# The first mixture's rows that go by DRAM: plain gathers into ring places and adds on VectorE in place of adding gathers

## The chip, the cores and the metric

The kernel runs on one core of a Trainium2 chip. The time is device microseconds of one execution. A core has TensorE (matrix products into PSUM), VectorE, ScalarE and GpSimd (called PE, DVE, ACT and POOL in the profile), SyncE (SP), which here issues most transfers, and sixteen DMA engines that all queues share. Every engine and every queue works through its own instructions in order and waits on semaphores for the others.

## What is computed

Two transformer blocks follow one another on 512 rows of width 1024: in each a mixer, then a mixture of experts, then a norm. The change is in the mixture of the first block: every row picks one of 4 groups and in it 2 of 8 experts, so there are 32 experts of width 256.

```python
combine = jnp.sum(jax.nn.one_hot(global_idx, N_EXPERTS, dtype=jnp.float32) * weights[..., None], axis=1)
y = jnp.zeros_like(x2d)
for e in range(N_EXPERTS):
    h = jax.nn.silu(x2d @ w_gate[e]) * (x2d @ w_up[e])
    y = y + combine[:, e:e + 1] * (h @ w_down[e])
```

The block's output is its input plus y.

## The kernel before, in words

`moe1` computes this mixture. Experts go in pairs, 16 units of two; each expert has 64 slots for rows, so a unit fills 128 partitions. Unit u gathers its rows from DRAM (L1596), turns them by transposes (L1609), multiplies them by its gate and up matrices (L1711), takes silu on ScalarE (L1714) and the product on VectorE (L1715), transposes the result (L1765, copied at L1766) and, one unit later in the code, multiplies it by the down matrices (L1655). Two matrices of each kind, 1 MB each, are loaded per unit, 96 MB in all. The residual `h` lies in SBUF as four tiles of 128 rows.

A unit's result rows reach `h` in one of two ways:

- By TensorE: `down` splits the rows into a high part (ScalarE, L1785) and a low part (VectorE, L1786), and `scatter` multiplies a one-hot matrix (L1790) by them (L1806, L1807) and adds the outcome to `h` on VectorE (L1800), half a tile at a time, through two PSUM banks in turn.
- By DRAM: `by_dram` scales the rows on ScalarE (L1664), and an indirect DMA of GpSimd's queue writes them to their places in a DRAM buffer `yd` (L1665), which is zeroed early in the first mixer (L503). After the last such unit eight indirect DMAs (L1730, one for each of the two choices of each of the four tiles) read rows of `yd` and add them to `h` in flight. A row whose expert is not among these units has an index out of bounds, and nothing is moved for it.

`FROM` (the first expert by DRAM, 8) and `BYDRAM` (20 experts) make units 4 to 13 go by DRAM.

The matrices come through a ring of places of 1 MB. Its parts have 6, 6, 3 and 2 places; `mo.cycle` says which part each next load takes, 17 loads to a cycle, and `place` takes a place outside of the cycle. Within a part the places go round. A load is issued on SyncE's queue, and it waits there, with all that is queued behind it, until its place has been read for the last time. A planner orders the instructions of each engine by its own model of when things are ready, so the order on a queue can differ from the code.

After unit 15 comes a loop for extra rounds (L1589), for experts that got more rows than they have slots. It starts with a meeting of all engines and queues. The down product of unit 15 and the last scatters come behind it.

```python
for u in range(mo.U):
    ...
    if prev and prev[0] in far:
        by_dram(*prev)
```

Of the kernel before, what the change touches and what calls it, by code (L numbers as in the profile page):

```python
# [16 lines left out]
T = 512  # L17
# [9 lines left out]

FROM = {1: 8, 2: 0}
BYDRAM = {1: 20, 2: 14}
# [153 lines left out]
class Kern:  # L183
# [259 lines left out]
    def mixer1(self, after):  # L443
# [52 lines left out]
        for step in "R00 R01 P0 R10 R11 A0 P1 R20 R21 A1 P2 R30 R31 A2 P3 A3".split():  # L496
            kind, j = step[0], int(step[1])
            if kind == "P":
                qkv[j] = self.sb_proj(pp, sp, j, xh, xl)
                if j == 2:  # L500
                    self.yd = tc.dram_tile([ZROW[1], D], F32, name="yd1")
                    zeros = qkv[j][0][64:128, 0]
                    nc.sync.dma_start(self.yd.rearrange("(p a) (d c) -> p (a d) c", p=64, c=T),  # L503
                                      zeros[:, None, :].to_broadcast([64, ZROW[1] // 32, T]))
                if j == 3:
                    wo = shift_pools()
            elif kind == "A":
                self.sb_attn(sp, j, qkv.pop(j), o, ("sb",))
            else:
                g = int(step[2])  # L510
                unit = self.rw_unit(up, j, g, S[g], o, AR, bt, kt, vch, xg, g2, TTc, PC)
                next(unit)
                drain(before)
                next(unit)
                before = unit
                if (j, g) == (3, 1):
                    drain(unit)
                    cA.close()
# [909 lines left out]
    def places(self, rp, mo):  # L1428
# [10 lines left out]
        nc.vector.tensor_tensor(rw, rw, mo.pos, OP.add)  # L1439
        nc.vector.tensor_tensor(rw, rw, ov, OP.add)  # L1440
        if mo.which == 2:
            nc.vector.tensor_scalar(mo.row, rw, float(ZROW[2]), None, op0=OP.min)
            return
        nc.vector.tensor_copy(mo.row, rw)

# [197 lines left out]
    def moe1(self):  # L1643
# [34 lines left out]
        def body(num, wts, idx, first):  # L1678
# [14 lines left out]
            for u in range(mo.U):  # L1693
# [3 lines left out]
                last = u == mo.U - 1  # L1697
                if last and first:
                    SC = self.place(mo, 2, R32)
                    y14 = down(prev[1], [self.moe_next(mo) for _ in range(2)], wts[:, u - 1:u], onehot(u - 1, SC[:, 0:T]),  # L1700
# [26 lines left out]
                if far and u == far[-1] + 1:  # L1727
                    for c in range(2):
                        for n in range(NT):
                            nc.gpsimd.indirect_dma_start(  # L1730
                                out=self.h[:, n], out_offset=None, in_=self.yd,
                                in_offset=bass.IndirectOffsetOnAxis(ap=mo.row[:, n, c:c + 1], axis=0),
                                bounds_check=ZROW[1] - 1, oob_is_err=False, compute_op=OP.add)
                hT = gp.tile([128, 2, 128], F32, name="hT", bufs=1)
# [48 lines left out]
    def rows_hl(self, oh, ol, p, w):  # L1783

        self.last = self.nc.scalar.activation(oh, p, AF.Copy, scale=w)  # L1785
        self.lo = self.nc.vector.scalar_tensor_tensor(ol, p, w, oh, op0=OP.mult, op1=OP.subtract)  # L1786

    def onehot(self, SC, mo, num, u):
# [37 lines left out]
    def moe2(self, out):  # L1826
        nc, tc, mo = self.nc, self.tc, self.mo
        with mo.cx, mo.cr:
# [48 lines left out]
            def body(num, wts, idx, first):  # L1877
# [50 lines left out]
                if first:  # L1928
                    back = [self.moe_slot(mo) for _ in range(NT)]
                    for n in range(NT):  # L1930
                        for c in range(2):
                            nc.gpsimd.indirect_dma_start(
                                out=back[n][:, c * D:c * D + D], out_offset=None, in_=self.yd,
                                in_offset=bass.IndirectOffsetOnAxis(ap=mo.row[:, n, c:c + 1], axis=0),
                                bounds_check=ZROW[2], oob_is_err=False)
                g = self.moe_slot(mo)[:, 0:D]
# [103 lines left out]
```

## Time and profile before

| | us |
|---|---|
| median of 3 runs | 1421.97 (1419.99 to 1422.15) |
| the profiled execution, its own time | 1419.69 |
| its span | 1417.9 |
| TensorE busy | 1289.0 (91%) |
| VectorE busy | 841.6 (59%) |
| ScalarE busy | 701.6 (49%) |
| GpSimd busy | 410.2 (29%) |

The durations below come from the one profiled execution; its time stands 2.28 us under the median. Times on its axis count from the start of the span. The mixture of the first block lies between about 460 and 722 us. "busy" counts instructions only: the landing of a DMA is told apart, and a row in brackets says how long the engine was idle before and what ended it. DMA share is the mean busy share of the sixteen DMA engines. PEclk is the granted clock of TensorE as a share of 2.4 GHz.

### The profile page before, as it was taken

How to read it: one execution, taken by the hardware profiler on the slowest of the kernel's cores; microseconds unless marked ns; L12 is line 12 of the kernel's file. 1: busy time of each engine (PE TensorE's matmuls, PEld its weight loads, DVE VectorE, ACT ScalarE, POOL GpSimd, SP SyncE). 2: the span in 40 equal slices, each digit the busy share in tenths (PEclk: the TensorE clock that was granted, in tenths of full speed). 3: DMA queues.
4: the chain of work that ended last, by engine and by line, in shares of the span. 5: the costliest groups of instructions: out<-in, count | busy, mean ns of one | idle time of the engine just before them, and what ended most of it. 6: DMA issues, size and time to landing. Idle time of an engine off the chain costs nothing.

```text
span 1417.9 us, 20482 instructions
## 1 busy us (share of the span) xinstructions
PE 1289.0 (91%) x7792; PEld 927.7 (65%) x7792; DVE 841.6 (59%) x1432; ACT 701.6 (49%) x1217; POOL 410.2 (29%) x329
## 2 busy tenths in 40 slices
PE   7999999999897999999379999999996999999993
PEld 5777766767696555554156776777894666666662
DVE  4679866566656131000075656657637799998895
ACT  6433433334634221211064555555545788888883
POOL 1000224241104101110366102011124555555445
PEclk9999999999998899999789999999997999999996
DMA  5232440000484999999832121202386999889943
GB/s 189 75 89 75 107 109 2 1 1 2 188 330 170 386 419 419 418 418 422 223 101 75 30 76 45 86 24 100 105 334 209 321 360 382 320 332 391 385 166 125
DMA packets 54452, 283.93 MB, mean 200 GB/s; under 512 B 8849, under 2 KB 9745, under 8 KB 28738
## 3 DMA queue, kind: packets, MB, share of 16 engines
q1 hardware_dynamic: 43634, 254.75, 47.9%
q0 software_dynamic: 9840, 26.39, 5.8%
q8 instruction: 66, 1.08, 0.3%
q10 hardware_dynamic: 864, 1.31, 0.3%
q14 instruction: 48, 0.39, 0.1%
HBM read 270.70 MB, written 22.29 MB: 207 GB/s over the span
## 4 chain that ended last, share of the span: by engine, by line
PE 68%; DVE 13%; DMA 11%; ACT 3%; issue 2%; POOL 1%; SPq 0%; DVEq 0%; POOLq 0%; ACTq 0%
PE mm L322 12%; PE ua L1903 4%; PE ua L1901 4%; PE ua L1902 4%; PE mm L1711 4%; DMA ew<-in_e1down_dram 3%; DMA ew<-in_e1up_dram 3%; PE ua L1655 2%; PE sb L322 2%; PE sb L1844 2%; PE sb L1843 2%; PE sb L1845 2%; PE sb L715 2%; DMA ew<-in_e1gate_dram 2%; DVE elo L1625 2%
## 5 line engine op out<-in xcount | busy, mean ns | idle before, releaser
L1625 DVE TENSOR_TENSOR elo<-ew,ehi 128x1024 fp32r<-128x1024 f32 x147 | 231.1, 1614 | 32.9 <-ACT ehi L1624 22.6
L1624 ACT ACTIVATE ehi<-ew 128x1024 fp32r<-128x1024 f32 x192 | 203.0, 1061 | 62.7 <-PE ua L1902 37.2
L322 PE MATMUL mm<-xh,whi 128*128 128x512 f32 (+1 forms) x384 | 155.9, 406 | 4.0 <-DVE hq L1143 3.7
L322 PE MATMUL mm<-xl,whi 128*128 128x512 f32 (+1 forms) x384 | 154.0, 401 | 0.5 <-DVE xl L354 0.3
L322 PE MATMUL mm<-xh,wlo 128*128 128x512 f32 (+1 forms) x384 | 152.8, 398 | 0.0
L1625 POOL TENSOR_TENSOR elo<-ew,ehi 128x1024 fp32r<-128x1024 f32 x45 | 125.9, 2799 | 64.8 <-ACT ehi L1624 63.0
L1711 PE MATMUL mm<-ew,xTh 128*64 128x256 f32 x1024 | 119.2, 386 | 6.4 <-DMA ew<-in_e1up_dram 4.7
L1903 PE MATMUL ua<-elo,xTh 128*96 128x512 f32 x256 | 102.9, 402 | 8.5 <-DVE elo L1625 8.4
L1711 PEld LDWEIGHTS mm<-ew,xTh 128*64 128x64 f32 x1024 | 73.5, 139 | 47.5 <-DMA ew<-in_e1up_dram 6.4
L1715 DVE TENSOR_TENSOR hh<-hh,mm 128x256 f32<-128x256 f32 x16 | 6.7, 421 | 163.5 <-ACT hh L1714 163.5
L1901 PE MATMUL ua<-ehi,xTh 128*96 128x512 f32 x256 | 102.3, 399 | 0.7 <-ACT xTh L1613 0.6
L1902 PE MATMUL ua<-ehi,xTl 128*96 128x512 f32 x256 | 101.8, 398 | 0.0
L296 ACT ACTIVATE whi<-w 128x1024 fp32r<-128x1024 f32 x53 | 55.9, 1057 | 91.1 <-PE mm L322 72.5
L297 DVE TENSOR_TENSOR wlo<-w,whi 128x1024 fp32r<-128x1024 f32 x52 | 63.7, 1227 | 51.7 <-ACT whi L296 51.5
L1596 POOL DMA_INDIRECT xg<-xd,idx x32 | 36.7, 1147 | 196.2 <-PE sb L1609 123.7
L322 PEld LDWEIGHTS mm<-xh,whi 128*128 128x128 f32 x384 | 73.4, 191 | 23.2 <-DVE hq L1143 5.4
L322 PEld LDWEIGHTS mm<-xl,whi 128*128 128x128 f32 x384 | 73.7, 192 | 16.7 <-issue 3.5
L322 PEld LDWEIGHTS mm<-xh,wlo 128*128 128x128 f32 x384 | 73.6, 192 | 16.0 <-issue 2.2
L1655 PE MATMUL ua<-ew,hT 128*64 128x512 f32 x240 | 66.4, 600 | 1.2 <-ACT hT L1766 1.1
L1714 ACT ACTIVATE hh<-mm 128x256 f32<-128x256 f32 x16 | 6.1, 383 | 112.8 <-PE mm L1711 112.8
L1903 PEld LDWEIGHTS ua<-elo,xTh 128*96 128x96 f32 x256 | 41.9, 164 | 30.6 <-DVE elo L1625 11.2
L1167 POOL TENSOR_TENSOR hAT<-hAT,hmt 128x512 f32<-128x512 f32 x16 | 22.1, 1381 | 118.9 <-DVE hmt L1166 118.3
(640 smaller groups left out, 3028.0 us busy)
## 6 DMA issues: line engine op xcount, KB each, us to landing
ew<-in_e1up_dram SPq DMA_DIRECT2D x32, 1024.0 KB, 17.8
ew<-in_e2up_dram SPq DMA_DIRECT2D x32, 1024.0 KB, 8.3
ew<-in_e2gate_dram SPq DMA_DIRECT2D x32, 1024.0 KB, 9.2
ew<-in_e2down_dram SPq DMA_DIRECT2D x32, 1024.0 KB, 12.5
ew<-in_e1gate_dram SPq DMA_DIRECT2D x31, 1024.0 KB, 19.5
ew<-in_e1down_dram SPq DMA_DIRECT2D x30, 1024.0 KB, 20.6
w<-in_win_dram SPq DMA_DIRECT2D x53, 512.0 KB, 3.6
ew<-in_wout_dram SPq DMA_DIRECT2D x8, 1024.0 KB, 6.9
```

The costliest lines, as they stand in the source:

```text
L296: nc.scalar.activation(hi, s, AF.Copy)
L297: (eng or nc.vector).tensor_tensor(lo, s, hi, OP.subtract)
L322: mm = lambda w, x, start=False, stop=False: nc.tensor.matmul(p[:, s], w[:, k], x[:, k, s], start=start, stop=stop, skip_group_check=parts ...
L715: nc.tensor.matmul(po[d, 0:128], v[:, kb, d], wT[hh][:, kb * 128:(kb + 1) * 128], start=kb == 0, stop=kb == b)
L1596: return self.nc.gpsimd.indirect_dma_start(out=xg, out_offset=None, in_=mo.xd, in_offset=bass.IndirectOffsetOnAxis(ap=idx[:, u:u + 1], axi ...
L1624: self.hi = nc.scalar.activation(hi, s, AF.Copy)
L1625: self.lo = (nc.gpsimd if pool else nc.vector).tensor_tensor(lo, s, hi, OP.subtract)
L1655: nc.tensor.matmul(p[hs(a)], hT[:, k, hs(a)], w[a][:, k * 1024 + d * 512:k * 1024 + d * 512 + 512], start=k == 0, stop=k == 1)
L1711: nc.tensor.matmul(d[hs(a)], xT[:, k, hs(a)], w[2 * m + a][:, k * 256:k * 256 + 256], start=k == 0, stop=k == KD - 1)
L1901: nc.tensor.matmul(p, xh[:, kk], hi[:, s], start=kk == 0, stop=False)
L1902: nc.tensor.matmul(p, xl[:, kk], hi[:, s], start=False, stop=False)
L1903: nc.tensor.matmul(p, xh[:, kk], lo[:, s], start=False, stop=kk == KD - 1)
```

## The change

`FROM` of the first mixture becomes 6, so units 3 to 12 go by DRAM and unit 13 goes by TensorE; the number of units on each way is as before. `yd` gets one row more, which two small DMAs set to zero, and an index out of bounds is clamped to that row (`places`), so all rows are moved. The return is taken over by `back`, which the second mixture now shares: plain gathers, each into half of a landing tile. In the first mixture the landing tiles are two places of ring part 2 and two of ring part 3, taken in unit 13. In unit 14 VectorE adds both halves of each tile to `h`. The scatter of unit 13 stands ahead of unit 14's down product.

```diff
-FROM = {1: 8, 2: 0}
+FROM = {1: 6, 2: 0}
...
-                    self.yd = tc.dram_tile([ZROW[1], D], F32, name="yd1")
+                    self.yd = tc.dram_tile([ZROW[1] + 1, D], F32, name="yd1")
                     zeros = qkv[j][0][64:128, 0]
-                    nc.sync.dma_start(self.yd.rearrange("(p a) (d c) -> p (a d) c", p=64, c=T),
+                    for d in range(2):
+                        nc.sync.dma_start(self.yd[ZROW[1]:ZROW[1] + 1, T * d:T * d + T], zeros[0:1])
+                    nc.sync.dma_start(self.yd[0:ZROW[1]].rearrange("(p a) (d c) -> p (a d) c", p=64, c=T),
                                       zeros[:, None, :].to_broadcast([64, ZROW[1] // 32, T]))
...
+        nc.vector.tensor_scalar(mo.row, rw, float(ZROW[mo.which]), None, op0=OP.min)
         if mo.which == 2:
-            nc.vector.tensor_scalar(mo.row, rw, float(ZROW[2]), None, op0=OP.min)
             return
-        nc.vector.tensor_copy(mo.row, rw)
...
                 if last and first:
+                    self.scatter(ys[-1:], 0)
+                    self.scatter(ys[-1:], 1)
...
                 if far and u == far[-1] + 1:
-                    for c in range(2):
-                        for n in range(NT):
-                            nc.gpsimd.indirect_dma_start(
-                                out=self.h[:, n], out_offset=None, in_=self.yd,
-                                in_offset=bass.IndirectOffsetOnAxis(ap=mo.row[:, n, c:c + 1], axis=0),
-                                bounds_check=ZROW[1] - 1, oob_is_err=False, compute_op=OP.add)
+                    back = self.back(mo, [self.place(mo, i) for i in (2, 2, 3, 3)])
+                if far and u == far[-1] + 2:
+                    for n in range(NT):
+                        for c in range(2):
+                            nc.vector.tensor_tensor(self.h[:, n], self.h[:, n], back[n][:, c * D:c * D + D], OP.add)
...
+    def back(self, mo, tiles):
+
+        for n, t in enumerate(tiles):
+            for c in range(2):
+                self.nc.gpsimd.indirect_dma_start(
+                    out=t[:, c * D:c * D + D], out_offset=None, in_=self.yd,
+                    in_offset=bass.IndirectOffsetOnAxis(ap=mo.row[:, n, c:c + 1], axis=0),
+                    bounds_check=ZROW[mo.which], oob_is_err=False)
+        return tiles
```

SyncE's queue, the loads of the last units before (the names are ring places of part 0 to 3 with a running number; DMAHW and DMASW are the semaphores of transfers issued by SyncE and by GpSimd): the down pair of unit 12, gate, up and down of the units 14 and 13, the down pair of unit 14, gate of unit 15.

```order
L1540 DMA ew2_5659<-in_e1down_dram 128x2048 [waits DMAHW2_49,PE_49]
L1540 DMA ew2_5661<-in_e1down_dram 128x2048 [waits DMAHW3_49,PE_49]
L1540 DMA ew2_5684<-in_e1gate_dram 128x2048 [waits DMAHW4_49,PE_49]
L1540 DMA ew3_5686<-in_e1gate_dram 128x2048 [waits DMAHW5_49,PE_49]
L1540 DMA ew0_5688<-in_e1up_dram 128x2048 [waits DMAHW6_49,PE_49]
L1540 DMA ew0_5690<-in_e1up_dram 128x2048 [waits DMAHW7_49,PE_49]
L1540 DMA ew0_5741<-in_e1down_dram 128x2048 [waits DMAHW0_49,PE_49]
L1540 DMA ew0_5743<-in_e1down_dram 128x2048 [waits DMAHW1_49,PE_49]
L1540 DMA ew1_5791<-in_e1down_dram 128x2048 [waits DMAHW2_49,PE_49]
L1540 DMA ew1_5793<-in_e1down_dram 128x2048 [waits DMAHW3_49,PE_49]
L1540 DMA ew1_5811<-in_e1gate_dram 128x2048 [waits DMAHW4_49,PE_49]
```

The same place on SyncE now, again from the down pair of unit 12 to the first gate matrix of unit 15.

```order
L1541 DMA ew2_5643<-in_e1down_dram 128x2048 [waits DMAHW4_49,PE_49]
L1541 DMA ew2_5645<-in_e1down_dram 128x2048 [waits DMAHW5_49,PE_49]
L1541 DMA ew0_5700<-in_e1up_dram 128x2048 [waits DMAHW6_49,PE_49]
L1541 DMA ew0_5702<-in_e1up_dram 128x2048 [waits DMAHW7_49,PE_49]
L1541 DMA ew0_5753<-in_e1down_dram 128x2048 [waits DMAHW0_49,PE_49]
L1541 DMA ew0_5755<-in_e1down_dram 128x2048 [waits DMAHW1_49,PE_49]
L1541 DMA ew2_5696<-in_e1gate_dram 128x2048 [waits DMAHW5_49,DMAHW2_49,PE_49]
L1541 DMA ew1_5821<-in_e1down_dram 128x2048 [waits DMAHW3_49]
L1541 DMA ew1_5823<-in_e1down_dram 128x2048 [waits DMAHW4_49]
L1541 DMA ew3_5698<-in_e1gate_dram 128x2048 [waits DMASW2_49,DMASW1_49,DVE_49]
L1541 DMA ew1_5841<-in_e1gate_dram 128x2048 [waits DMAHW6_49]
```

Unit 14's two gate matrices moved behind its up matrices and the down pair of unit 13; the first (part 2) waits for the load and the use of the second down matrix of unit 12, whose place it takes (5645), the second (part 3) for two gathers and VectorE, which are the writers and the reader of the third landing tile (5665).

VectorE before, from unit 13's product to unit 15's, with the one-hots, the low parts and a small copy between.

```order
L1715 TENSOR_TENSOR hh_5643<-hh_5643,mm_5610 128x256 [waits Activation_49]
L1790 TENSOR_SCALAR ew2_5790<-io512_4406,num_3848 128x512 [waits DMAHW2_49,DMAHW1_49,DMAHW7_49,DMAHW0_49,PE_49]
L1790 TENSOR_SCALAR ew2_5790<-io512_4406,num_3848 128x512
L1715 TENSOR_TENSOR hh_5725<-hh_5725,mm_5692 128x256 [waits Activation_49]
L1746 COPY ew2_5855<-wts_3849 128x1 [waits DMAHW4_49,DMAHW3_49,DMASW2_49]
L1786 SCALAR_TENSOR_TENSOR ew2_5796<-ua_5797,wts_3849,ew2_5796 128x512 [waits DMAHW3_49,Activation_49]
L1786 SCALAR_TENSOR_TENSOR ew2_5796<-ua_5804,wts_3849,ew2_5796 128x512 [waits Activation_49]
L1715 TENSOR_TENSOR hh_5852<-hh_5852,mm_5819 128x256 [waits Activation_49]
```

VectorE now, from the first add after unit 13's product (5663 to 5666 are the four landing tiles; 1802 is the one-hot, 1788 the low part, 1812 the eviction of a scatter).

```order
L1735 TENSOR_TENSOR h_3258<-h_3258,ew2_5663 128x1024 [waits DMASW5_49]
L1735 TENSOR_TENSOR h_3258<-h_3258,ew2_5663 128x1024 [waits DMASW6_49,DVE_49]
L1802 TENSOR_SCALAR ew2_5820<-io512_4408,num_3850 128x512 [waits DMAHW4_49,DMAHW3_49,DMAHW5_49,DMASW2_49,DVE_49]
L1735 TENSOR_TENSOR h_3258<-h_3258,ew2_5664 128x1024 [waits DMASW7_49]
L1802 TENSOR_SCALAR ew2_5820<-io512_4408,num_3850 128x512
L1735 TENSOR_TENSOR h_3258<-h_3258,ew2_5664 128x1024 [waits DMASW0_49,DVE_49]
L1788 SCALAR_TENSOR_TENSOR oh0_5759<-ua_5760,wts_3851,oh0_5759 128x512 [waits Activation_49]
L1735 TENSOR_TENSOR h_3258<-h_3258,ew3_5665 128x1024 [waits DMASW1_49]
L1788 SCALAR_TENSOR_TENSOR oh1_5767<-ua_5768,wts_3851,oh1_5767 128x512 [waits DMASW4_49,DMASW2_49,Activation_49]
L1735 TENSOR_TENSOR h_3258<-h_3258,ew3_5665 128x1024 [waits DMASW2_49,DVE_49]
L1735 TENSOR_TENSOR h_3258<-h_3258,ew3_5666 128x1024 [waits DMASW3_49]
L1812 TENSOR_TENSOR h_3258<-h_3258,ch_5788 128x512 [waits PE_49]
```

The eight adds stand ahead of unit 14's product, which comes after the evictions of unit 13's scatter; the last add follows this first eviction.

TensorE now, the scatter of unit 13 (the banks ch and pq) and the gate product of unit 14, whose second matrix is 5698.

```order
L1819 MATMUL ch_5788<-oh0_5759,SC_5757 128x512 [waits DVE_49]
L1819 MATMUL pq_5792<-oh0_5759,SC_5757 128x512
L1818 MATMUL ch_5796<-oh0_5759,SC_5757 128x512 [waits DVE_49]
L1819 MATMUL ch_5796<-oh0_5759,SC_5757 128x512
L1818 MATMUL pq_5800<-oh0_5759,SC_5757 128x512 [waits DVE_49]
L1819 MATMUL pq_5800<-oh0_5759,SC_5757 128x512
L1818 MATMUL ch_5804<-oh1_5767,SC_5757 128x512 [waits DVE_49,Activation_49]
L1819 MATMUL ch_5804<-oh1_5767,SC_5757 128x512
L1818 MATMUL pq_5808<-oh1_5767,SC_5757 128x512 [waits DVE_49]
L1819 MATMUL pq_5808<-oh1_5767,SC_5757 128x512
L1818 MATMUL ch_5812<-oh1_5767,SC_5757 128x512 [waits DVE_49]
L1714 MATMUL mm_5704<-ew3_5698,xTh_5630 64x256 [waits DMAHW5_49]
```

Before, unit 14's gate and up products stood ahead of unit 13's down product, and no scatter stood between; now they come behind it and behind six and a half of the eight scatters of unit 13.

## Rows read from the trace of the kernel before

**Rows 1.** Busy time by stretches: stretch, us, engines busy (instructions), granted clock, DMA share, GB/s.

```profile
660.00:680.00 20.00, 16.42 (x94) 7.82 (x90) 1.41 (x4) 3.40 (x6) 1.18 (x2) 1.00 1.00 418
680.00:700.00 20.00, 7.78 (x64) 4.60 (x64) 0.99 (x2) 0.77 (x2) 12.22 (x8) 0.84 0.93 227
```

**Rows 2.** The chain that ended last, 670 to 715 us: start, us, what.

```profile
675.07 7.85 DMA yd<-ot,out
...
687.53 19.46 DMA h<-yd,row
707.00 1.62 issue
708.62 6.25 PE ua L1655 x16
```

**Rows 3.** Timeline of TensorE and ScalarE: start, us, engine, line, instruction, count, idle before.

```profile
654.59 3.65 PE L1655 MATMUL ua<-ew,hT 128*64 128x512 f32 x12
...
675.12 3.94 PE L1655 MATMUL ua<-ew,hT 128*64 128x512 f32 x16 [1.05 <-ACT hT L1766]
...
690.58 0.44 PE L1765 MATMUL sb<-pc_c,hh 128*128 128x128 f32 x2 [0.93 <-DVE hh L1715]
...
689.69 0.38 ACT L1714 ACTIVATE hh<-mm 128x256 f32<-128x256 f32 x1 [9.90 <-PE mm L1711]
691.06 0.38 ACT L1766 ACTIVATE ew<-sb 128x256 f32<-128x256 f32 x1 [0.98 <-PE sb L1765]
```

**Rows 4.** Timeline of GpSimd: unit 12's rows to DRAM, the first adding gather.

```profile
659.23 0.97 POOL L1665 DMA_INDIRECT yd<-ot,out  x1 [15.23 <-ACT hT L1766]
...
683.70 1.63 POOL L1730 DMA_INDIRECT h<-yd,row  x1 [7.65 <-DMA yd<-ot,out]
685.64 1.59 POOL L1730 DMA_INDIRECT h<-yd,row  x1 [0.31 <-issue]
```

**Rows 5.** Timeline of SyncE's queue: unit 14's gate pair, unit 15's down pair.

```profile
634.05 3.51 SPq L1540 DMA_DIRECT2D ew<-in_e1gate_dram  x2
...
667.97 2.80 SPq L1540 DMA_DIRECT2D ew<-in_e1down_dram  x2
```

**Rows 6.** Issue to landing: lines L1665, L1596, L1932 (second mixture's return); page, 512 KB loads.

```profile
DMA to landing us min/median/max: 7.8/8.2/11.1
...
DMA to landing us min/median/max: 4.1/8.6/10.1
...
DMA to landing us min/median/max: 4.6/5.5/10.9
...
w<-in_win_dram SPq DMA_DIRECT2D x53, 512.0 KB, 3.6
```

**Rows 7.** Timeline of the second mixture's end: two plain gathers, VectorE beside them.

```profile
1371.09 7.54 POOL L1932 DMA_INDIRECT ew<-yd,row  x1 [0.30 <-DVE ew L1786]
1378.94 0.99 POOL L1932 DMA_INDIRECT ew<-yd,row  x1 [0.30 <-issue]
...
1370.88 8.04 DVE L1625 TENSOR_TENSOR elo<-ew,ehi 128x1024 fp32r<-128x1024 f32 x7
...
1398.61 1.21 DVE L1956 TENSOR_TENSOR h<-h,ew 128x1024 f32<-128x1024 f32 x1
```

**Rows 8.** Timeline of VectorE: one-hot halves, low part, eviction.

```profile
657.43 0.88 DVE L1790 TENSOR_SCALAR ew<-io,num 128x512 fp32r<-128x512 f32 x2 [4.39 <-PE ua L1655]
678.69 0.75 DVE L1786 SCALAR_TENSOR_TENSOR ew<-ua,wts,ew 128x512 fp32r<-128x512 f32 x1 [9.47 <-ACT ew L1785]
...
717.91 0.69 DVE L1800 TENSOR_TENSOR h<-h,pq 128x512 f32<-128x512 f32 x1 [0.24 <-PE pq L1807]
```

**Rows 9.** TensorE's gate and up products of units 0 and 1; stretch with low clock.

```profile
463.97 9.16 PE L1711 MATMUL mm<-ew,xTh 128*64 128x256 f32 x64
...
474.77 7.13 PE L1711 MATMUL mm<-ew,xTh 128*64 128x256 f32 x64
...
694.00:696.00 2.00, 0.00 (x0) 0.00 (x0) 0.00 (x0) 0.00 (x0) 0.97 (x2) 0.50 0.96 164
```

**Rows 10.** Busy time by stretches, the first mixer.

```profile
160.00:320.00 160.00, 153.92 (x1253) 106.84 (x1250) 101.42 (x223) 54.85 (x120) 60.17 (x92) 1.00 0.19 45
```

More of the change, by code (lines that the diff above doesn't have):

```diff
@@ L1928, in body @@
                 if first:
[L1929 to L1935, printed above, removed]
+                    back = self.back(mo, [self.moe_slot(mo) for _ in range(NT)])
                 g = self.moe_slot(mo)[:, 0:D]
```

## The prediction

> **What bounds the kernel now.** I read the busy time by stretches first, because the average over the span hides what limits this stage. Up to 680 us the sixteen DMA engines are full (share 1.00, 418 GB/s) and TensorE works beside them; after 680 us the traffic falls to 227 GB/s and TensorE does 7.78 us of work in 20 [rows 1]. Then the chain that ended last: its pieces there are the landing of the last scatter to DRAM (7.85 us), the adding gathers (19.46 us), 1.62 us without a cause that the profile shows, and the down product of unit 15 at 708.62 [rows 2]. In the order of instructions the piece of 1.62 us is the meeting of all engines ahead of the loop for extra rounds. The timeline says how long the engines were ready by then: unit 15 has its silu at 689.69 and its last transposes at 690.58, and their copy ends at 691.06 + 0.38 = 691.44 [rows 3]. So 708.62 - 691.44 = 17.2 us is the price of eight gathers that run alone. The first starts at 683.70 [rows 4].
>
> **What the change removes.** The return by eight adding gathers (1.63 us and 0.31 us of pause each, [rows 4]) no longer ends the stage: it moves one unit earlier (units 3 to 12 instead of 4 to 13), nothing is added in the DMA, and eight plain gathers take its place. Were that all, up to 17.2 us would go. It isn't all.
>
> **What it adds: a wait in the load queue.** The four landing tiles are ring places of parts 2 and 3. Part 2 has three places and part 3 has two, so the loads that come next there, the two gate matrices of unit 14, lose their free places. In the built order of SyncE the first is issued only after TensorE has used up unit 12's second down matrix, and the second waits for the fifth and sixth gather and for VectorE's adds of them; queued behind it are the gate, up and down matrices of unit 15 (6 MB) and the 512 KB of w_in2. Before, both were issued from 634.05 on, and the last of the down pair behind them from 667.97 on [rows 5]. So I add up the chain that now ends in VectorE's sixth add.
>
> 1. Up to unit 12's down product the loads have the same order, so its time stays: the twelve matmuls from 654.59 last 3.65 us, to 658.24 [rows 3], and its rows are sent at 659.23 [rows 4].
> 2. Landing in DRAM: 7.8 to 11.1 us, median 8.2 [rows 6]. The loads in flight (up 14, down 13, then gate 14 first half and down 14) keep the engines full as before; I take 8.2, to 667.4.
> 3. The first gather came 0.8 us after the landing (683.70 against 675.07 + 7.85, [rows 2, 4]): 668.2.
> 4. A plain gather took 0.99 us with 0.30 us of pause [rows 7]: the sixth is issued at 674.7, the eighth at 677.2.
> 5. From issue to landing: median 5.5 us where the second mixture does this same return, 8.6 us for the row gathers beside full loads [rows 6]. The loads run out at about 673: before, unit 15's up pair was in half of 7.13 us ahead of the silu at 689.69 [rows 3, 9], and 5 MB of what had come by then is now stuck, 12.5 us at 418 GB/s. The gathers fly on both sides of that, so I take 7: first row tile at 675.2, sixth at 681.7, eighth at 684.2.
> 6. VectorE holds up more than the landings: 6 adds of 1.21 us [rows 7], two one-hot halves in 0.88 us and two low parts of 0.75 us [rows 8] stand between in its order, 9.6 us together: the sixth add ends at 684.8. Only now is the second gate matrix issued. A load of 512 KB lands in 3.6 us [rows 6]; with 0.5 MB more at 418 GB/s, 4.9 us is my estimate for 1 MB, so 689.7.
> 7. TensorE starts unit 14's gate even later, since its order puts seven scatters of unit 13 ahead, which use two banks in turn. They wait for VectorE's seventh add (1.21), one eviction (0.69, [rows 8]), the eighth add (1.21), then further evictions and pairs of matmuls, some 3.7 us: 691.6.
> 8. What follows is TensorE's own work: gate and up of units 14 and 15 (2 x 7.13, [rows 9]), the down product of unit 14 (3.94) and its transposes (0.44, [rows 3]), the rest of the scatter (0.9, estimated as three of those matmuls), and 1.4 us for unit 14's silu, product and copy, which now have no other unit's work ahead of them: 20.9 us.
> 9. The clock: after TensorE had stopped at 691.0 the granted clock was 0.50 between 694 and 696, the 1.2 GHz level [rows 9]. From 669 on TensorE will have little to do, so I let unit 14 start at that level. The first unit of this mixture began in that state and took 9.16 us where the next took 7.13 [rows 9]: 2.0 us.
> 10. From the silu to the last copy 1.75 us as before (689.69 to 691.44, [rows 3]), and the 1.62 us of the meeting [rows 2].
>
> Sum: 691.6 + 20.9 + 2.0 + 1.75 + 1.62 = 717.9, against 708.62: +9.3 us. One thing comes back: unit 15's down product took 6.25 us after the long pause and the same 16 matmuls 3.94 us in unit 14 [rows 2, 3]; TensorE is now warm there, -2.3 us. This leaves +7.0.
>
> **Who is held while POOL and VectorE meet.** The seventh and eighth gather are issued while VectorE adds. In the second mixture one gather took 7.54 us instead of 0.99 while seven two-input subtractions ran back to back on VectorE for 8.04 us [rows 7]; the next one, after that row of subtractions, took 0.99. So this costs 0 to 6.5 us. Here the adds are spaced by landings and by one-hots, so I take 1.0: +8.0 in all. The Trainium skill ("SBUF — State Buffer", section "Who interferes with whom") says that a two-input VectorE instruction shares only its second read with GpSimd, and infers that generating descriptors isn't held by it; by that this term is 0 and the sum +7.0. The row of 7.54 us speaks against that inference, so I keep the row's upper end.
>
> **What costs nothing.** Loads are not the end: 7.5 MB from 684.8 on are in by about 705, ahead of TensorE. The 4.2 MB of the gathers (8 x 128 x 1024 x 4 bytes) run where loads are stuck anyway. Eight more half-tile evictions (unit 2 and unit 13 are now scattered alone) are 5.5 us of VectorE; those of unit 2 lie in a stretch where it is nearly idle, those of unit 13 are in step 7. The zero row adds two small DMAs at about 162 us. They also make the planner interleave the first mixer otherwise, between about 152 and 320 us. TensorE is idle there for 160 - 153.9 = 6.1 us in all [rows 10], so I allow 2 us either way and take 0.
>
> **The rivals.** (a) Faster: TensorE catches up and the loads set the end. This is so if the sixth add ends before 684.8 - 8.0 = 676.8, which wants the sixth tile 1 us after its issue; or if the place is free without the adds. Then unit 15 ends as before, later only by the gathers' bytes (10 us at 418 GB/s): 691.44 + 10 + 1.62 - 2.3 is 7.9 us under 708.62. Against it: the shortest landing is 4.1 us [rows 6]. (b) No change: all short ends at once, landing in DRAM 7.8, gathers 4.6, no hold, no silu wait: -0.4 - 2.4 - 1.0 - 1.4 = -5.2, so +2.8, within the limit if the first mixer gives 1 us back. (c) Slower still: POOL is held by the adds as in the row of 7.54 us, 5.5 us more: +13.5. The step that decides is VectorE never waiting between adds while gathers seven and eight are pending. (d) The change doesn't take the gathers off the end: the order shows them ahead of the last unit, so I give this no chance of its own.
>
> **How the numbers follow.** The profiled execution took 1419.69 us (its span is 1417.9), 2.3 under the median of 1421.97; the forecast +8.0 gives 1427.7 in its terms and 1430.0 against the median. Rival (a) gives 1414.1, (b) about 1424, (c) 1435.5. Chances: forecast 0.52 (1425 to 1433), (c) 0.26, (b) 0.13, (a) 0.09. The low end of the range takes in (b) with the 2 us of the first mixer, 1422; the high end takes in (c) with a landing of 9 us, both mixers' 2 us included, 1439. Left out are (a) and the tails, about 0.15. A measurement here tells a change from none at about 0.2% (2.8 us): faster 0.09, same 0.13, slower 0.78.
>
> **What would show it.** In the profile after, the adds should run from about 675 to 688, the load of unit 14's second gate matrix should wait for VectorE to about 685, the traffic should fall well under 418 GB/s for some microseconds before 685, TensorE should take up unit 14's gate at about 692 at the low clock, and the last down product should start at about 718 without a pause for gathers. I am wrong if the gate load is issued before the adds, if unit 15's up matrices land after TensorE is ready for them, or if gathers seven and eight take more than 1.5 us each.

## The result and the profile after

| | before | after |
|---|---|---|
| median, us | 1421.38 (4 runs, 1419.99 to 1422.15) | 1431.47 (4 runs, 1430.27 to 1432.36) |
| the profiled execution, its own time | 1419.69 | 1432.04 |
| its span | 1417.9 | 1430.3 |

The change makes the kernel slower by 10.1 us: ratio 1.0073, 95% interval 1.0058 to 1.0088. The forecast was 1430.0.

The same stretches as in [rows 1], with one more (stretch, us, engines busy, granted clock, DMA share, GB/s):

```profile
660.00:680.00 20.00, 11.55 (x34) 3.35 (x31) 1.26 (x2) 3.51 (x6) 6.75 (x7) 0.86 0.81 296
680.00:700.00 20.00, 10.96 (x59) 6.32 (x61) 14.06 (x17) 0.00 (x0) 3.10 (x3) 0.63 0.92 356
700.00:720.00 20.00, 14.82 (x105) 9.81 (x101) 3.60 (x7) 3.96 (x7) 0.68 (x1) 0.97 0.53 200
```

Before, the DMA engines were full to 680 us and TensorE did 16.42 us of work in the first of these stretches [rows 1]; now the traffic there falls to 296 GB/s, TensorE does 11.55 us, and all but two matmuls of the gate and up products of units 14 and 15 run after 694 us. (Below, "down 15" stands for the down product of unit 15, "gate 14" for the gate product of unit 14, and so on.)

TensorE around it (start, us, instruction, count, idle time before and what ended it): unit 12's down product, two scatters of unit 13, gate and up of unit 14, unit 15's transposes and down product. Compare [rows 3].

```profile
658.98 3.65 PE L1656 MATMUL ua<-ew,hT 128*64 128x512 f32 x12
...
685.10 0.80 PE L1819 MATMUL ch<-oh,SC 128*128 128x512 f32 x1 [10.38 <-DVE oh L1788]
...
689.75 0.79 PE L1818 MATMUL ch<-oh,SC 128*128 128x512 f32 x1 [3.43 <-DVE h L1812]
...
694.93 7.12 PE L1714 MATMUL mm<-ew,xTh 128*64 128x256 f32 x62
...
715.31 0.44 PE L1767 MATMUL sb<-pc_c,hh 128*128 128x128 f32 x2 [0.93 <-DVE hh L1718]
721.69 5.50 PE L1656 MATMUL ua<-ew,ew 128*64 128x512 f32 x16 [5.94 <-POOL ew L1757]
```

GpSimd: unit 12's rows, and the first, sixth and eighth gather (compare [rows 4]).

```profile
663.62 0.97 POOL L1666 DMA_INDIRECT yd<-ot,out  x1 [15.47 <-ACT hT L1768]
672.69 1.03 POOL L1794 DMA_INDIRECT ew<-yd,row  x1 [8.10 <-DMA yd<-ot,out]
...
679.23 1.50 POOL L1794 DMA_INDIRECT ew<-yd,row  x1 [0.30 <-issue]
...
682.35 1.35 POOL L1794 DMA_INDIRECT ew<-yd,row  x1 [0.30 <-issue]
```

VectorE: the first two additions, the third, the sixth and seventh, an eviction, the eighth.

```profile
678.64 2.55 DVE L1735 TENSOR_TENSOR h<-h,ew 128x1024 f32<-128x1024 f32 x2 [21.19 <-DMA ew<-yd,row]
...
681.63 1.22 DVE L1735 TENSOR_TENSOR h<-h,ew 128x1024 f32<-128x1024 f32 x1
...
686.75 2.35 DVE L1735 TENSOR_TENSOR h<-h,ew 128x1024 f32<-128x1024 f32 x2
689.01 0.68 DVE L1812 TENSOR_TENSOR h<-h,ch 128x512 f32<-128x512 f32 x1
689.61 1.22 DVE L1735 TENSOR_TENSOR h<-h,ew 128x1024 f32<-128x1024 f32 x1
```

SyncE's queue: unit 14's down pair, then nothing for 24 us, then the second gate matrix of unit 14 and the gate pair of unit 15 (compare [rows 5]).

```profile
663.03 0.90 SPq L1541 DMA_DIRECT2D ew<-in_e1down_dram  x2
687.99 1.28 SPq L1541 DMA_DIRECT2D ew<-in_e1gate_dram  x3
```

The sixth addition ends at about 687.95 (the row of two from 686.75 is 2.35 us long), and at 687.99 the held load is sent. TensorE's scatters wait 10.38 us for a low part that stands behind four additions on VectorE and 3.43 us more for an eviction that stands behind the next three; its gate product of unit 14 goes on at 694.93, right behind a scatter and without a wait for the load. So what gate 14 stood behind last were the scatters, as in step 7 of the prediction.

At the other end, 6.38 us lie between the last transposes (715.31) and the down product (721.69). The profile names a GpSimd instruction, whose result down 15 doesn't read. What TensorE's sequencer (PEldq in these rows) does there stands in its branch instructions at the loop (duration in ns, least, median, most; start of the first and the last), the kernel before first:

```profile
L1589 PEldq COMPARE_BRANCH  x3: 100/190/5383, 691.7 to 708.4; - x3
L1590 PEldq COMPARE_BRANCH  x3: 104/193/3644, 716.1 to 721.4; - x3
```

One of three, the second, takes 5.38 us before and 3.64 us after. Between 715.5 and 722 two DMA queues that the profile calls "instruction" move two packets each; in the changed kernel without the loop (below) they move none there. Before, the long branch started at 692.0 and lay under the wait for the gathers; now it starts at 716.4, with no wait left to lie under, and TensorE comes to its last branch at 721.4, 3.4 us after ScalarE as the last of the others (718.0). The Trainium skill ("Runtime: NRT & Kernel Launch", section "Instruction fetch mechanics") says that a taken branch out of the window of fetched pages forces a fetch of the target first; the rows agree with a fetch, and they give the time; that this branch leaves the window is not in the rows.

### The profile page after: what moved, and what is told of

The parts are those of the page before. It is cut to its first block, busy times and chain, and to the rows that moved or that the text cites. A ratio compares the mean times of both kernels' runs of the same rounds, so it can differ in the third digit from the quotient of the medians.

```text
span 1430.3 us, 20519 instructions
## 1 busy us (share of the span) xinstructions
PE 1299.8 (91%) x7792; PEld 933.2 (65%) x7792; DVE 856.6 (60%) x1448; ACT 701.6 (49%) x1217; POOL 407.1 (28%) x329
## 5 line engine op out<-in xcount | busy, mean ns | idle before, releaser
L322 PEld LDWEIGHTS mm<-xl,whi 128*128 128x128 f32 x384 | 73.8, 192 | 16.6 <-issue 3.1
L1656 PE MATMUL ua<-ew,hT 128*64 128x512 f32 x240 | 71.9, 612 | 3.9 <-DMA ew<-in_e1down_dram 3.8
```

The costliest lines, as they stand in the source:

```text
L322: mm = lambda w, x, start=False, stop=False: nc.tensor.matmul(p[:, s], w[:, k], x[:, k, s], start=start, stop=stop, skip_group_check=parts ...
L1656: nc.tensor.matmul(p[hs(a)], hT[:, k, hs(a)], w[a][:, k * 1024 + d * 512:k * 1024 + d * 512 + 512], start=k == 0, stop=k == 1)
```

## The experiments

All times are medians; the kernel before stood at 1421.5 to 1421.9 us in these comparisons.

### The zero row

The row alone, on the kernel before:

```diff
-                    self.yd = tc.dram_tile([ZROW[1], D], F32, name="yd1")
+                    self.yd = tc.dram_tile([ZROW[1] + 1, D], F32, name="yd1")
+                    for d in range(2):
+                        nc.sync.dma_start(self.yd[ZROW[1]:ZROW[1] + 1, T * d:T * d + T], zeros[0:1])
```

> The kernel before with one part of the change alone: the row of zeros behind the rows in DRAM, two small DMAs on SyncE's queue, and the clamp of the row numbers that goes with it; the gathers still add. Theory (the profile of after has the units' first matmuls 2.4 to 3.5 us later than before, from the first mixer on): the small DMAs and the order that the planner then gives to the first mixer cost that, so 1423.8 to 1424.9 us, and the stage around the gathers looks as it did before. Rival (the later starts are the scatter of single executions): 1421.4 us, within 1 us of the kernel before.

And the changed kernel without the two small DMAs:

```diff
-                    self.yd = tc.dram_tile([ZROW[1] + 1, D], F32, name="yd1")
+                    self.yd = tc.dram_tile([ZROW[1] + 64, D], F32, name="yd1")
-                    for d in range(2):
-                        nc.sync.dma_start(self.yd[ZROW[1]:ZROW[1] + 1, T * d:T * d + T], zeros[0:1])
-                    nc.sync.dma_start(self.yd[0:ZROW[1]].rearrange("(p a) (d c) -> p (a d) c", p=64, c=T),
-                                      zeros[:, None, :].to_broadcast([64, ZROW[1] // 32, T]))
+                    nc.sync.dma_start(self.yd.rearrange("(p a) (d c) -> p (a d) c", p=64, c=T),
+                                      zeros[:, None, :].to_broadcast([64, ZROW[1] // 32 + 2, T]))
```

> The changed kernel with its zeros laid down by one DMA over 64 more rows in place of the two small ones, so that no instruction is added in the first mixer. Theory (the small DMAs and their order cost 2.4 to 3.5 us there): 1428 to 1429 us. Rival (scatter): 1431.5 us, as the changed kernel.

Measured 1421.85 us (ratio 1.0000, 0.9991 to 1.0009) and 1430.74 us (1.0057, 1.0043 to 1.0071; the changed kernel's interval overlaps). The theory falls: the row costs nothing that these runs can tell. (The clamp that the first expectation names isn't in that edit; the changed kernel has it.) In the first one's profile unit 12's down product also starts 3.6 us later than in [rows 3], at 658.23, while the time is that of the kernel before. Two kernels below without any zero row, the move alone and the kernel before without the loop, start it at 658.02 and 658.73, and all eleven other profiles lie between 656.98 and 659.08. So 654.59 in [rows 3] is the odd one, and later starts up to there are no loss of the change.

### The held load

Landing places taken behind unit 14's loads:

```diff
+                if far and u == far[-1] + 2:
+                    back = self.back(mo, [self.place(mo, i) for i in (2, 2, 3, 3)])
                 p = self.ps("gu")
...
-                if far and u == far[-1] + 1:
-                    back = self.back(mo, [self.place(mo, i) for i in (2, 2, 3, 3)])
```

> The changed kernel, but its landing places are taken from the rings behind unit 14's four weight loads, so that no load of units 14 and 15 waits for an addition; gathers and additions are the same. Theory (the second gate load of unit 14, held until the sixth addition ended, set TensorE's resumption): unit 14's gate and up matmuls run at about 674 to 682, ahead of the scatters, which still stand behind the eight additions on VectorE (end about 690); then down 14 (3.6), gate and up 15 (7.1) and the ending of 7.3: TensorE starts down 15 at 712 to 716 in place of 721.7, so 1422 to 1427 us. Rival (the chain rows, eight gathers, eight additions in itself sets the end, loads or no loads): 1431 us, unchanged within 1.

Measured 1444.68 us (1.0150, 1.0136 to 1.0164): 13 us slower than the changed kernel, which neither theory had. No load is held any more, and gate and up of unit 14 run from 662.19 on. But TensorE stops at 673.4, because unit 14's product stands behind five additions on VectorE, and the additions come at a pace of 3.7 us (TensorE: first part of down 13, unit 14's transposes; VectorE: first and eighth addition):

```profile
671.48 1.90 PE L1656 MATMUL ua<-ew,hT 128*64 128x512 f32 x4
697.08 0.69 PE L1767 MATMUL sb<-pc_c,hh 128*128 128x128 f32 x2 [23.70 <-DVE hh L1720]
...
680.47 1.23 DVE L1735 TENSOR_TENSOR h<-h,ew 128x1024 f32<-128x1024 f32 x1 [23.82 <-DMA ew<-yd,row]
...
705.24 1.23 DVE L1735 TENSOR_TENSOR h<-h,ew 128x1024 f32<-128x1024 f32 x1 [1.35 <-DMA ew<-yd,row]
```

The pace is that of the landings (issue to landing of the gathers, least, median, most: the changed kernel, this one, and the move alone, below):

```profile
DMA to landing us min/median/max: 5.9/6.2/6.2
...
DMA to landing us min/median/max: 8.6/17.1/24.2
...
DMA to landing us min/median/max: 9.9/14.6/16.9
```

The gathers are issued at the same times as in the changed kernel (671.86 to 680.98 against 672.69 to 682.35), and land 17.1 us after their issue in the median, not 6.2, since loads stand in the other queue all the while (the down pairs landed 24.8 us after theirs, and the DMA engines were full, with 412 GB/s from 680 to 690). The hold that I took for the loss had also cleared the way for the gathers. The Trainium skill ("DMA: Bandwidth & Descriptors", section "Queues, rings and completion order") says that a DMA engine serves its queues in turn, a packet at a time; by that a gather shares with queued loads. The landings here agree; no row here shows the order of the packets.

### Additions out of the way

The same, with the additions written at the end of unit 15:

```diff
                 nc.vector.tensor_tensor(hh, hh, p[:, 256:512], OP.mult)
+                if far and last:
+                    for n in range(NT):
+                        for c in range(2):
+                            nc.vector.tensor_tensor(self.h[:, n], self.h[:, n], back[n][:, c * D:c * D + D], OP.add)
                 if last:
                     break
...
-                if far and u == far[-1] + 2:
-                    for n in range(NT):
-                        for c in range(2):
-                            nc.vector.tensor_tensor(self.h[:, n], self.h[:, n], back[n][:, c * D:c * D + D], OP.add)
```

> As the kernel with the late places, and the eight additions written behind the scatters of units 12 to 14, at the end of unit 15, so that neither loads nor scatters wait for them all. Theory (held loads and held scatters are what the gathers cost): TensorE runs on from down 13 through unit 15 and waits only for what is left of the additions (end about 690), down 15 starts at 698 to 704, the time is 1408 to 1415 us, under both kernels. Rival (VectorE's one chain decides: scatters' and gathers' additions are both on it and unit 15's product is behind them): down 15 at about 708 to 712, 1418 to 1422 us.

Measured 1421.22 us (0.9996, 0.9986 to 1.0005): 23.5 us less than with the additions ahead of unit 14's product and unit 13's scatters, with the gathers landing as late (median 17.0). TensorE works on to 700 us with one wait over 2 us (2.87 us, for a load), and the rival holds at the end: unit 15's product stands behind the last addition, which waits for its landing, and the branch comes after that (TensorE: last transposes, down 15; VectorE: the last three additions, the product).

```profile
706.47 0.69 PE L1767 MATMUL sb<-pc_c,hh 128*128 128x128 f32 x2 [6.46 <-DVEq L1590]
712.67 5.43 PE L1656 MATMUL ua<-ew,ew 128*64 128x512 f32 x16 [5.51 <-DMA ew<-in_fin_g_dram]
...
702.22 2.36 DVE L1724 TENSOR_TENSOR h<-h,ew 128x1024 f32<-128x1024 f32 x2 [6.06 <-DMA ew<-yd,row]
704.80 1.23 DVE L1724 TENSOR_TENSOR h<-h,ew 128x1024 f32<-128x1024 f32 x1 [0.21 <-DMA ew<-yd,row]
...
706.00 0.41 DVE L1720 TENSOR_TENSOR hh<-hh,mm 128x256 f32<-128x256 f32 x1
```

So I wrote the eight additions behind the last loads of the body and put the last three of them behind the product:

```diff
+            for n in range(NT):
+                for c in range(2):
+                    add = nc.vector.tensor_tensor(self.h[:, n], self.h[:, n], back[n][:, c * D:c * D + D], OP.add)
+                    if 2 * n + c > 4:
+                        self.behind(add.ins, prod.ins.name)
```

> As the kernel with the additions at the end, and the last three of the eight placed behind unit 15's product on VectorE, so that TensorE's last transposes and its branch over the loop do not wait for the last gathers. Theory (TensorE's branch takes 3.4 to 3.7 us wherever it comes, and the meeting of the engines needs the last gather landed, about 705): transposes at 701, the branch lies under the gathers' landing, down 15 starts at 707 to 709 in place of 712.7, 1415.5 to 1418 us. Rival (the branch starts only after the meeting): down 15 at 711 to 713, 1420 to 1421 us.

Measured 1415.95 us (0.9962, 0.9947 to 0.9977): faster than both kernels. The transposes run at 701.40, the branch lies under the landings, and down 15 starts at 708.12, 1.5 us after the last addition ends.

```profile
701.40 0.44 PE L1768 MATMUL sb<-pc_c,hh 128*128 128x128 f32 x2 [0.93 <-DVE hh L1720]
708.12 6.30 PE L1656 MATMUL ua<-ew,ew 128*64 128x512 f32 x16 [6.28 <-issue]
...
700.92 0.42 DVE L1720 TENSOR_TENSOR hh<-hh,mm 128x256 f32<-128x256 f32 x1 [4.07 <-ACT hh L1719]
...
705.37 1.23 DVE L1760 TENSOR_TENSOR h<-h,ew 128x1024 f32<-128x1024 f32 x1 [1.22 <-DMA ew<-yd,row]
```

### A held load alone

The changed kernel's places, and the additions behind unit 13's scatters:

```diff
                     self.scatter(ys[-1:], 1)
+                    for n in range(NT):
+                        for c in range(2):
+                            nc.vector.tensor_tensor(self.h[:, n], self.h[:, n], back[n][:, c * D:c * D + D], OP.add)
...
-                if far and u == far[-1] + 2:
-                    for n in range(NT):
-                        for c in range(2):
-                            nc.vector.tensor_tensor(self.h[:, n], self.h[:, n], back[n][:, c * D:c * D + D], OP.add)
```

> The changed kernel with the landing places as they are, so that one gate load of unit 14 still waits for an addition, and the eight additions written behind unit 13's scatters, so that no scatter waits for them (the planner then sends unit 15's loads and matmuls ahead of the held load). Theory (the held load is enough to set the end, the scatters behind the additions are not needed for it): gathers contend with unit 15's loads, the additions end at about 700 to 704, the held load lands 3 to 4 us later, and unit 14's half of gate and up, down 14 and the ending of 7 us follow: down 15 at 718 to 724, 1428 to 1435 us. Rival (the scatters behind the additions set it): down 15 at 708 to 714, 1417 to 1423 us.

Measured 1431.28 us (1.0065, 1.0051 to 1.0078), the changed kernel's time. No scatter waits for an addition, unit 15's loads go first, and the one held gate matrix is sent at 697.40 and lets TensorE stand 7.80 us; down 15 starts at 722.59. (SyncE: unit 15's up pair, the held load; TensorE: unit 14, down 15.)

```profile
663.94 1.19 SPq L1541 DMA_DIRECT2D ew<-in_e1up_dram  x2
697.40 0.33 SPq L1541 DMA_DIRECT2D ew<-in_e1gate_dram  x1
...
702.45 9.54 PE L1717 MATMUL mm<-ew,xTh 128*64 128x256 f32 x64 [7.80 <-DMA ew<-in_e1gate_dram]
...
722.59 5.82 PE L1656 MATMUL ua<-ew,ew 128*64 128x512 f32 x16 [5.11 <-DMA ew<-in_fin_g_dram]
```

So the loss stays with the load held and no scatter behind an addition, and it stays (and grows) with the scatters and unit 14's product behind additions and no load held (the late places). In both runs the gathers also land later than in the changed kernel, in 15.6 and 17.1 us against 6.2, since loads run beside them. What either wait would cost by itself, with landings of 6.2 us, no run shows.

### The move and the replacement apart

The kernel before with units 3 to 12 by DRAM, still with adding gathers:

```diff
-FROM = {1: 8, 2: 0}
+FROM = {1: 6, 2: 0}
...
                 if last and first:
+                    self.scatter(ys[-1:], 0)
+                    self.scatter(ys[-1:], 1)
```

> The kernel before with the move alone: units 3 to 12 go by DRAM in place of 4 to 13, so that unit 13 is scattered; the gathers still add, into the sum h itself. Theory (the hold of loads and the plain gathers are the loss; the move in itself lets the chain rows, gathers start one unit, about 12 us, earlier): first gather at about 672 in place of 684, the last lands by 700 to 705 beside the loads in place of 707, time 1412 to 1420 us. Rival (the move is the loss: one more unit's scatters stand behind the gathers on h): TensorE starts down 15 at 715 or later, 1428 us or more.

Measured 1439.97 us (1.0133, 1.0116 to 1.0151): the rival. The gathers do start at 671.84, but they land in 14.6 us (median) where it was 7.8 in the kernel before, the fifth waits for the first (both add to the same tile), and unit 13's scatters wait 19.09 us for `h`:

```profile
699.62 0.79 PE L1808 MATMUL ch<-oh,SC 128*128 128x512 f32 x1 [19.09 <-DVE h L1802]
...
677.54 1.56 POOL L1732 DMA_INDIRECT h<-yd,row  x1 [0.30 <-DVE oh L1788]
682.50 1.55 POOL L1732 DMA_INDIRECT h<-yd,row  x1 [3.40 <-DMA h<-yd,row]
```

So of the two parts the move costs 18.5 us and the replacement, on top of it, gives 8.5 back. The replacement without the move, with four places of ring part 0 as landing tiles and the additions behind unit 15's product:

```diff
-FROM = {1: 6, 2: 0}
+FROM = {1: 8, 2: 0}
...
-                    self.scatter(ys[-1:], 0)
-                    self.scatter(ys[-1:], 1)
...
+                if far and u == far[-1] + 2:
+                    back = self.back(mo, [self.place(mo, i) for i in (0, 0, 0, 0)])
...
-                    back = self.back(mo, [self.place(mo, i) for i in (2, 2, 3, 3)])
...
+                    self.behind(add.ins, prod.ins.name)
```

> The replacement without the move: units 4 to 13 go by DRAM as in the kernel before, unit 13 is not scattered, and the rows come back by plain gathers into four places of the largest ring, which nothing loads into any more, with all eight additions behind unit 15's product on VectorE. Theory (the move is the loss, the replacement a gain): gathers from about 685 at 1.3 us each, with the loads nearly done beside them, the last landed by 701 to 703 in place of 707, the branch hidden under them, TensorE starts down 15 at 704 to 706 in place of 708.6: 1416.5 to 1419.5 us. Rival (the replacement is neutral or a loss where it stands, 4 MB in place of about 2.7): 1421 to 1426 us.

Measured 1417.91 us (0.9980, 0.9971 to 0.9989), 3.7 us faster. The time is as expected, the place is not: the landings took 11.9 us in the median, seven additions ran to 711.8, and down 15 started at 712.32, later than the 708.62 of [rows 2].

```profile
712.32 5.23 PE L1656 MATMUL ua<-ew,ew 128*64 128x512 f32 x16 [17.90 <-DVEq L1590]
...
695.84 1.22 DVE L1758 TENSOR_TENSOR h<-h,ew 128x1024 f32<-128x1024 f32 x1 [1.91 <-DMA ew<-yd,row]
700.89 10.92 DVE L1758 TENSOR_TENSOR h<-h,ew 128x1024 f32<-128x1024 f32 x7 [3.83 <-DMA ew<-yd,row]
```

The rows show no gain in the mixture. Its last eviction starts at 725.24, and at 724.76 in the run with the zero row alone, whose time is that of the kernel before. Most of the gain lies in the second mixer, behind a pause in which TensorE waits 2.9 us for VectorE, and it is TensorE's clock: the same 24 matmuls after it take 8.4 us in the kernel before (from 779.58) and 5.6 us here (from 781.57), since the granted clock fell to 0.50 there (the 1.2 GHz level) and stayed at 1.00 here (the kernel before first; stretch, us, engines busy, granted clock, DMA share, GB/s):

```profile
780.00:785.00 5.00, 5.00 (x13) 3.89 (x13) 4.17 (x8) 1.99 (x3) 0.00 (x0) 0.50 0.30 75
782.00:787.00 5.00, 5.00 (x24) 4.12 (x23) 4.16 (x8) 1.99 (x3) 0.00 (x0) 1.00 0.30 82
```

So the theory got its time for another reason, and the rival's first half (neutral where it stands) fits the rows. Why the clock fell in one and not in the other stays open. The stretch took 8.4 us in the changed kernel too, in both runs on the zero row and in the one with the additions behind the scatters, so the 10.1 us don't hang on it. It took 6.9 to 7.2 us in the other six: some 1.4 us of the gain with the additions behind the product, and 1.2 to 1.3 us of what the two kernels without the loop save, lie there.

### The loop

Both kernels without the loop for extra rounds in the first mixture (`end` is given for that one alone):

```diff
-        ex = nc.values_load(mo.extra[0:1, 0:1], min_val=0, max_val=-(-T // mo.cap) - 1)
-        with tc.For_i(0, ex, 1): ...
+        if not end:
+            ex = nc.values_load(mo.extra[0:1, 0:1], min_val=0, max_val=-(-T // mo.cap) - 1)
+            with tc.For_i(0, ex, 1): ...
```

> The changed kernel without the loop over extra rounds in the first mixture (left out: the rounds beyond the first, the meeting of the engines before them and TensorE's branch over them). Theory (7.3 us lie between unit 15's last transposes' copy and TensorE's down 15, of which 3.6 are the branch): about 5 to 7 us saved, 1424.5 to 1426.5 us. Rival (a meeting of 1.6 us as in the kernel before is all of it): 1429 to 1430 us.

> The kernel before without the loop over extra rounds in the first mixture (left out: the same as in the last kernel). Theory (TensorE's branch ran under the wait for the adding gathers and cost nothing; the meeting cost 1.6 us and held down 15, 6.3 us, behind the gathers, which without it can run under them): 3 to 8 us saved, 1413.5 to 1418.5 us. Rival (the branch costs the same in both kernels): 5 to 7 us saved, the same as in the changed kernel, with down 15 behind the gathers' landing as before.

Measured 1422.25 us (1.0008, 0.9998 to 1.0017) and 1408.75 us (0.9914, 0.9897 to 0.9931). In the changed kernel the loop, its meeting included, costs 9.2 us: 0.92 us now lie between the last transposes and down 15, and its 16 matmuls take 3.65 us, not 5.50.

```profile
714.57 0.44 PE L1768 MATMUL sb<-pc_c,hh 128*128 128x128 f32 x2 [0.93 <-DVE hh L1719]
715.49 3.65 PE L1657 MATMUL ua<-ew,ew 128*64 128x512 f32 x16 [0.47 <-ACT ew L1769]
```

In the kernel before it costs 12.7 us, most of it since without the meeting down 15 and the first scatters run under the gathers, and only short waits for `h` are left (3.40 us and 3.57 us):

```profile
693.12 0.44 PE L1766 MATMUL sb<-pc_c,hh 128*128 128x128 f32 x2 [0.93 <-DVE hh L1716]
694.03 4.23 PE L1656 MATMUL ua<-ew,ew 128*64 128x512 f32 x16 [0.47 <-ACT ew L1767]
...
705.58 0.50 PE L1807 MATMUL ch<-ew,ew 128*128 128x512 f32 x1 [3.40 <-DVE h L1801]
```

So the branch is a term of the stage, but not the reason of the loss: without the loop the two kernels stand 13.5 us apart, not 10.1.

## Why the prediction was right, point by point

The sign, the time (1430.0 against 1431.47) and the mechanism held: a load queue held by VectorE's sixth addition, scatters of unit 13 behind the additions, and TensorE's work of two units behind both. The steps:

- **Step 1** (unit 12's down product keeps its time) was 4.4 us off: it ended at 658.98 + 3.65 = 662.63. The run with the zero row alone has 3.6 of this at no cost in time, and no other profile starts as early as the one that I read, so most of it is the difference of single executions.
- **Steps 2 to 6** held. From the sending of the rows to the first gather 9.07 us (forecast 8.97), gathers land in 5.9 to 6.2 us (forecast 7), from the first gather to the sixth addition's end 15.3 us (forecast 16.6), and the load is sent then and not before.
- **Step 7** held: gate 14 starts 7.0 us after that addition (forecast 6.8).
- **Step 9** (2.0 us of low clock) failed. The granted clock was 0.63 from 680 to 700, but the scatters bore it; gate and up of unit 14 took 7.12 us. From gate 14 to the last transposes it took 20.4 us, where steps 8 and 9 with the silu gave 23.8.
- **Step 10** was mis-sized: 6.38 us from the transposes to down 15 against 0.86 + 1.62. I took the meeting from a trace in which the branch was hidden. The part that I gave back for the warm clock was 0.75 us and not 2.3: down 15 took 5.50 us after the pause.
- **GpSimd's hold**: 0.51 us at the sixth and 0.36 at the eighth gather, 0.9 of the 1.0 taken; none of it lengthens the chain, since VectorE waits for no gather behind the first. Rival (c) fell, though the sign that it named came true: VectorE doesn't wait between the additions from 678.64 to 690.8, and gathers seven and eight are issued in that time, in 1.02 and 1.35 us. The reason given for the 1.0, additions spaced by landings, failed with it. The last section has what the rows show of the hold.

Steps 8 and 9 were 3.4 us too long, step 10 and the warm clock 5.4 us too short, steps 2 to 7 with the hold 2.1 us too long. Behind step 1 the errors cancel to within 0.1 us, and that is luck: the mechanism was right, the sizes of its later terms were not. What step 1 missed is left: the profiled executions stand 12.35 us apart, not 8.0. The one before lies 1.7 us under its median and the one after 0.6 us above, so the medians stand only 10.1 us apart, and the forecast, counted from a median, came within 1.5 us.

Rival (a) was wrong in its reason: with the places free the loads are not the end, since gathers beside queued loads take 17 us to land and the additions that wait for them hold TensorE; that kernel took 1444.68 us and not 1414.1. And the prediction's "up to 17.2 us would go" counts the earlier return as a gain; the move alone, with gathers that still add, loses 18.5 us: the scatters of unit 13, now behind the return, wait on the same `h`.

## What to carry to other kernels

A transfer that moves ahead of other work also moves into its traffic and ahead of it in each queue: list who then stands behind its consumer, on the queues of loads and on the engine that consumes it. A borrowed buffer place holds every load behind the one that needs it back; taking the hold away pays only if the consumers of the late data are also put behind the work that doesn't need them. Here that order (places behind the loads, additions written behind the scatters, the last three behind the last product) turned 10.1 us of loss into 5.5 us of gain, some 1.4 us of which is the clock in the second mixer. And a gain of a few microseconds is to be looked for in the trace where it was expected: the replacement alone had the expected time without it.

## What the runs showed of the hardware

- TensorE's branch over the loop took 3.3 to 5.9 us in all runs that have it, 5.9 in the replacement alone and 3.3 in the ones with the additions behind the product and behind the scatters; the other engines' branches took under 0.1 us.
- Eight plain gathers of 512 KB landed in 6.2 us (median) with the load queue held and in 17.1 us with it running; eight adding ones in 7.8 and 14.6 us.
- A plain gather of the changed kernel's first mixture took 0.99 to 1.03 us of GpSimd where no addition ran as it was sent. One sent during a two-input addition was done 0.85 to 0.91 us after that addition had ended, in this kernel and in the others where it happened: here the sixth at 679.23 + 1.50 = 680.73, the first addition at 678.64 + 1.22 = 679.86; the eighth at 683.70, the third addition at 682.85. In the second mixture one gather took 7.78 us while VectorE did seven two-input subtractions, and the next one 0.99, as in [rows 7]. The first two additions don't overlap (2.55 us for two of 1.22), the seven subtractions do (8.11 us for seven of about 1.2); whether that makes the difference isn't shown. The inference that the prediction cites from the Trainium skill ("SBUF — State Buffer", section "Who interferes with whom") isn't borne out in either place:

```profile
1382.17 7.78 POOL L1794 DMA_INDIRECT ew<-yd,row  x1 [0.30 <-issue]
1390.25 0.99 POOL L1794 DMA_INDIRECT ew<-yd,row  x1 [0.30 <-DVE elo L1626]
...
1382.15 8.11 DVE L1626 TENSOR_TENSOR elo<-ew,ehi 128x1024 fp32r<-128x1024 f32 x7
```
